# Turns into two other PSUM banks at the opening of the first chunk period, and another place in VectorE's order for the subtractions of the first up tiles

## The chip, the cores and the metric

The kernel runs on one core of a Trainium2 chip. A core has a TensorE (PE: matmuls and transposes, with its weight loads shown as PEld), a VectorE (DVE), a ScalarE (ACT), a GpSimd (POOL) and a SyncE (SP), which here issues the loads from HBM. Each engine works through its own queue in order; semaphores make one engine wait for another. TensorE writes to PSUM, which has eight banks of 128 x 512 fp32. The metric is the device time of one execution in microseconds (us); lower is better. The times before are the median of three runs, 1123.79 us (1122.62 to 1124.88).

## The reference, cut to what matters

One hybrid decoder layer for 256 tokens of width 2048, in fp32:

```
h   = RMSNorm(x)
p   = h @ w_in                              # heads of attention and of a gated recurrence
m   = concat[RMSNorm(attention), recurrence] @ w_out
x   = x + RMSNorm(m)                        # "x2" in the kernel
h   = RMSNorm(x)
u   = relu(h @ w_up)                        # 2048 -> 8192
y   = (u * u) @ w_down                      # 8192 -> 2048
out = x + RMSNorm(y)
```

The change lies behind the layer's first half: where `h` of the MLP is made from `x2`, where the first products with `w_up` start, and where the first products with `w_down` start.

## The kernel before, in words

**Precision.** Each fp32 matmul is done as three faster ones: a value is split in a high part (`whi`, a cast on ScalarE, L90 or L689) and a low part (`wlo`, the value less its high part, a subtraction on VectorE, L91 or L694). `three` and `product` then issue high x high, high x low and low x high. So every tile of weights passes through ScalarE and VectorE before TensorE can take it: a load on SP into a raw buffer, a cast, a subtraction.

**Turns.** TensorE needs activations with their features on the partitions. `turn_act` (and `turn`, `turn_sum`, which call it) transposes four 128 x 128 blocks into one PSUM bank (L637), ScalarE casts the bank to the high part (L639), and VectorE subtracts to get the low part (L640). `turn_u` does the same for `u`: transposes (L669), a square on ScalarE (L671), a cast (L673), a subtraction (L674). A bank is free for the next turn when its last reader is done: for `turn_act` the subtraction on VectorE, for `turn_u` the square on ScalarE.

**PSUM.** The eight banks have four tags: "pj" with three, "sc" with three, "tr" and "o" with one each. `bank(tag, bufs)` gives a bank of a tag; a matmul into it waits until it is free.

**An order written out by hand.** From the last quarter of the `w_out` product on, the program puts TensorE's queue, and then also VectorE's, ScalarE's and SP's, in exactly the order in which the Python code issues the instructions (`manual_schedule`). Where a line stands in the code is where its instruction stands in its engine's queue.

**The up opening (about 400 to 441 us).** `residual(tb)` makes `x2` for 128 tokens (block row `tb`) with its sums of squares; `scaled(tb, c)` (L704, VectorE) makes block `c` of the normed `h` of that row; `turn(tb, c)` turns it into `h2T[c]`. Meanwhile the first four tiles of `w_up` (numbers 0 to 3) are split: `cast_t(i, h)` casts half `h` of tile `i` (L689), `lo_t(i, h)` subtracts it (L694), and with the second half of tile `i` also issues the load of tile `i + 3` (L78), whose raw buffer is the one that tile `i` gives free: three raw buffers go round. `cast2(i)` and `lo2(i)` do both halves. TensorE meanwhile ends the last `w_out` product (`w3`), with the turns of row 0 between its pieces, and goes on with `part(tb, tile, kind)`: four matmuls of one row with one tile, of kind "hh" (high x high), "lh" or "hl" (high x the tile's low part), all from L730. Tile 3 is needed first by `part(0, 3, "hh")`, tile 4 by the `wide_step` loop behind this stretch (L111 to L113).

**The chunk opening (about 471 to 517 us).** From here the MLP runs in chunks of 1024 features. The up products of a chunk are combined from seven products of half size, whose inputs are sums of blocks of `h` (`turn_sum` with the names "s1" to "s4"; "s4" is written into one half of `h2T[0]` and `h2T[1]`, beside the "a11" half that the first products read). `period(ch, ...)` lists a chunk's segments. Each segment has its weights (`prepare` casts and subtracts them, two segments ahead), additions between weight tiles (`adds`, VectorE, L873), turns that stand ahead of its matmuls in TensorE's queue (`turns`), its matmuls (`product`, L869, or `down_half`, L111 to L113), and loads behind them. Before the first period `down_half(0, 0, 0)` has begun the first two sums of the down product in two "sc" banks. They stay in use until the other half of that product has been added (`dn[0][1]`, the third segment) and copied out.

The first period (`ch == 1`) opens with: the first segment (`m1_first[0]`), ahead of it two turns of "s4" and the turn of `u[1, 0]`; the second segment (`m1_first[1]`), ahead of it the turn of `u[1, 1]`; `dn[0][1]`; `m5[0]`, `m5[1]`; `dn[1][0]`; `m6[0]`, `m6[1]`; `dn[1][1]`. In VectorE's queue the "s4" subtractions stand behind the subtractions of the first three segments' weights and one addition.

Of the kernel before, what the change touches and what calls it, by code (L numbers as in the profile page):

```python
# [29 lines left out]
def tile_hybrid_layer(  # L30
# [36 lines left out]
    def nm(s):  # L67
        uid[0] += 1
        return f"{s}{uid[0]}"
# [564 lines left out]
    def turn_act(src, hi, lo, tag="sc", bufs=3):  # L634
        ps = bank(tag, bufs)
        for i in range(4):
            nc.tensor.transpose(ps[:, i * P:(i + 1) * P], src[:, i * P:(i + 1) * P], ident)  # L637
        ps = ps.rearrange("p (a t) -> p a t", a=4)
        nc.scalar.copy(out=hi, in_=ps)  # L639
        nc.vector.tensor_tensor(out=lo, in0=ps, in1=hi.bitcast(F32), op=ALU.subtract)  # L640

    def turn(tb, c):
        turn_act(hn[tb][:, c * 512:(c + 1) * 512], *(h2T[c][:, :, i, tb * P:(tb + 1) * P] for i in range(2)))

    for c in range(3):
        ch = load_wide(w_out_v, 0, c * 512)
# [19 lines left out]
    def turn_u(uT, cb, tb, u, tag, bufs):  # L666
        tp = bank(tag, bufs)
        for i in range(4):
            nc.tensor.transpose(tp[:, i * P:(i + 1) * P], u[:, i * P:(i + 1) * P], ident)  # L669
        u2 = upool.tile([P, 4, P], F32, tag="u2", name=nm("u2"), bufs=2)  # L670
        nc.scalar.activation(out=u2, in_=tp.rearrange("p (a t) -> p a t", a=4), func=AF.Square)  # L671
        hi, lo = (uT[cb][:, :, i, tb * P:(tb + 1) * P] for i in range(2))
        nc.scalar.copy(out=hi, in_=u2)  # L673
        nc.vector.tensor_tensor(out=lo, in0=u2, in1=hi.bitcast(F32), op=ALU.subtract)  # L674
# [16 lines left out]
    def lo_t(i, h):  # L691
        k = slice(2 * h, 2 * h + 2)
        hi, lo = up_w[i]
        nc.vector.tensor_tensor(out=lo[:, k], in0=up_raw[i][:, k], in1=hi[:, k].bitcast(F32), op=ALU.subtract)  # L694
        if h == 1:
            load_t(i + 3)
# [5 lines left out]
    def scaled(tb, c):  # L702
        cs = slice(c * 512, (c + 1) * 512)
        nc.vector.scalar_tensor_tensor(out=hn[tb][:, cs], in0=x2[tb][:, cs], scalar=rh[:, tb:tb + 1], in1=gpre[c],  # L704
                                       op0=ALU.mult, op1=ALU.mult)

    ch = load_wide(w_out_v, 0, 3 * 512, pieces=2)
# [18 lines left out]
    def part(tb, tile, kind):  # L726
        for kt in range(4 * tile, 4 * tile + 4):
            a = tok(h2T, kt, tb)[1 if kind == "lh" else 0]
            b = up_w[tile][1 if kind == "hl" else 0][:, kt % 4, :]
            nc.tensor.matmul(ps[tb], lhsT=a, rhs=b, start=kt == 0 and kind == "hh", stop=kt == NKT - 1 and kind == "hl")  # L730

    def cast2(i):
        cast_t(i, 0)
        cast_t(i, 1)

    def lo2(i):
        lo_t(i, 0)
        lo_t(i, 1)


    w3(0, 11)
    scaled(0, 0)
    scaled(0, 1)
    cast2(0)
    turn(0, 0)
    scaled(0, 2)
    w3(11, 13)
    turn(0, 1)
    cast2(1)
    scaled(0, 3)  # L750
    lo_t(0, 0)
    w3(13, 15)
    turn(0, 2)
    w3(15, 16)
    turn(0, 3)
    evac_post(3, 1, banks[1])
    lo_t(0, 1)
    cast2(2)
    uT = new_uT()
    ps += [bank("pj"), bank("pj")]  # L760
# [9 lines left out]
    scaled(1, 1)  # L770
    part(0, 0, "hl")
    part(0, 3, "hh")
    turn(1, 0)
    part(0, 3, "lh")
    scaled(1, 2)
# [3 lines left out]
    turn(1, 2)  # L779
    part(1, 1, "hh")  # L780
    turn(1, 3)
    lo2(1)
    part(1, 2, "hh")
    part(1, 3, "hh")
    for tile_ in range(4):
# [11 lines left out]
    def half(tb, h):  # L797
        return hn[tb][:, h * 1024:(h + 1) * 1024]
# [4 lines left out]
    def turn_sum(src, c, tag="sc", bufs=3):  # L803
        t = sums[src[0]]
        turn_act(src[1][:, c * 512:(c + 1) * 512], *(t(slice(4 * c, 4 * c + 4), i) for i in range(2)), tag, bufs)
# [135 lines left out]
    raws, banks3, us, uTs = {}, {}, {0: prev}, {0: uT}  # L941
# [45 lines left out]
        m1[1].act.append(lambda: copy_out(0, "a", ch))  # L987
        return m1

    def t(ch, cb, tb, dst, tag="sc"):  # L990
        return lambda: turn_u(uTs[dst], cb, tb, us[ch][cb, tb], tag, 3)

    def period(ch, m1_next):
        d = ch - 1
        m5 = [up_seg("X", ch, h, "b", lambda: sums["s1"], True) for h in range(2)]
        m6 = [up_seg("X", ch, h, "a", lambda: sums["s2"], False) for h in range(2)]
        m7 = [up_seg("P", ch, h, "a", lambda: sums["s3"], False) for h in range(2)]
        m3 = [up_seg("Q", ch, h, "b", lambda: sums["s4"], False) for h in range(2)]
        m4 = [up_seg("X", ch, h, "a", lambda: sums["a22"], False) for h in range(2)]
        m2 = [up_seg("R", ch, h, "c", lambda: sums["a12"], True) for h in range(2)]  # L1000
        dn = [[down_seg(d, c, h) for h in range(2)] for c in range(4)]
        if ch == 1:
            q = [None, m1_first[0], m1_first[1], dn[0][1], m5[0], m5[1], dn[1][0], m6[0], m6[1], dn[1][1],
                 m7[0], m7[1], dn[2][0], m3[0], m3[1], dn[2][1], m4[0], m4[1], m2[0], m2[1],
                 m1_next[0], dn[3][0], m1_next[1], dn[3][1]]
        else:
            q = [m5[0], m5[1], dn[0][0], m6[0], m6[1], dn[0][1], m7[0], m7[1], dn[1][0], m3[0], m3[1], dn[1][1],
                 m4[0], m4[1], dn[2][0], m2[0], m2[1], dn[2][1], m1_next[0], dn[3][0], m1_next[1], dn[3][1]]
        A, B, C = ((lambda b=b: banks3[b, ch]) for b in "abc")
        m5[1].act.append(lambda: copy_out(1, "b", ch))  # L1010
        m6[1].act.append(lambda: copy_out(2, "a", ch))
        m7[1].dve.append(comb(ch, (1, 1), ALU.subtract, lambda: scr[1], A))
        m7[1].act.append(relu_in_place(ch, (1, 1)))
        m3[1].dve.append(comb(ch, (1, 0), ALU.subtract, B, lambda: scr[2]))
        m3[1].act.append(relu_in_place(ch, (1, 0)))
        m4[1].act.append(lambda: relu_21(ch))
        m2[1].dve.append(comb(ch, (0, 0), ALU.add, C, lambda: scr[0]))
        m2[1].act.append(relu_in_place(ch, (0, 0)))

        def plus(to, frm, c, h):  # L1020
            return lambda: add(raws[to, c, h], raws[frm, c, h])

        nx = ch + 1


        if ch == 1:
            plan = [(1, "X", "P", ch, 0), (2, "X", "P", ch, 1), (3, "X", "Q", ch, 0), (4, "X", "Q", ch, 1),
                    (6, "P", "Q", ch, 0), (7, "P", "Q", ch, 1), (12, "X", "R", ch, 0), (14, "X", "R", ch, 1),
                    (19, "X", "P", nx, 0), (21, "P", "Q", nx, 0), (22, "X", "P", nx, 1), (23, "X", "Q", nx, 0)]
        else:  # L1030
            plan = [(1, "X", "Q", ch, 1), (2, "P", "Q", ch, 1), (8, "X", "R", ch, 0), (10, "X", "R", ch, 1)]
            if nx < NCH:
                plan += [(17, "X", "P", nx, 0), (19, "P", "Q", nx, 0), (20, "X", "P", nx, 1), (21, "X", "Q", nx, 0)]
        for k, to, frm, c, h in plan:
            q[k].adds.append(plus(to, frm, c, h))
        if ch == 1:
            q[1].turns += [lambda c=c: turn_sum(("s4", half(0, 0)), c) for c in range(2)]
            q[1].turns.append(t(d, 1, 0, d))
            q[2].turns.append(t(d, 1, 1, d))
            loads = [(1, "d", d, 1, 1), (4, "d", d, 2, 0), (7, "d", d, 2, 1),  # L1040
                     (8, "R", ch, 0), (9, "R", ch, 1), (10, "d", d, 3, 0), (11, "Q", nx, 0), (12, "Q", nx, 1),
                     (13, "d", d, 3, 1), (14, "X", nx, 0), (15, "X", nx, 1), (16, "P", nx, 0), (17, "P", nx, 1),
                     (19, "d", ch, 0, 0), (21, "d", ch, 0, 1)]
        else:
            q[0].turns += [t(d, 0, 0, d), t(d, 0, 1, d)]
            q[3].turns.append(t(d, 1, 0, d))
            q[4].turns.append(t(d, 1, 1, d))
            loads = [(0, "d", d, 1, 0), (3, "d", d, 1, 1), (5, "R", ch, 0), (6, "R", ch, 1), (6, "d", d, 2, 0),
                     (9, "d", d, 2, 1), (12, "d", d, 3, 0), (15, "d", d, 3, 1),
                     (17, "d", ch, 0, 0), (19, "d", ch, 0, 1)]  # L1050
            if nx < NCH:
                loads += [(8, "Q", nx, 0), (9, "Q", nx, 1), (11, "X", nx, 0), (12, "X", nx, 1), (14, "P", nx, 0),
                          (15, "P", nx, 1)]
        for k, name, *where in sorted(loads, key=lambda x: (x[0], x[1] == "d")):
            q[k].loads.append(lambda name=name, where=where: (load_down if name == "d" else load_up)(
                *(where if name == "d" else [name] + where)))
        return [x for x in q if x is not None], q
# [10 lines left out]
    for ch in range(1, NCH):  # L1068
        m1 = first_products(ch + 1) if ch < NCH - 1 else [None, None]
        part, q = period(ch, m1)  # L1070
# [96 lines left out]
```

## Time and profile before

| | before |
|---|---|
| median of three runs | 1123.79 us (1122.62 to 1124.88) |
| the profiled execution's own time | 1124.23 us |
| its span in the profile | 1122.5 us |
| mean granted clock of TensorE | 0.985 of full speed |
| HBM read, written | 204.51 MB, 4.19 MB |

The profile shows one execution. Times in its timeline are us from the span's start: start, duration, engine, line of the program, operation, output <- input, shape; in square brackets the idle time of that engine just before, and what ended it. Durations of grouped rows (x2, x4, ...) run from the first start to the last end. A stretch's row gives, in this order, its bounds, its length, the busy time of PE, PEld, DVE, ACT and POOL (with how many instructions), the granted clock of TensorE (1.00 is full speed), the DMA engines' share and GB/s; the rows of TensorE alone leave the other engines out. Matmuls overlap by a fraction of their length, so 24 of them take less time than 24 times the duration of one.

### The profile page before, as it was taken

Reading aid. Unit: us, or ns where it says so; the run is one execution under the profiler, and the core shown is the slowest. Engines: PE = TensorE matmul, PEld = TensorE weight load, DVE = VectorE, ACT = ScalarE, POOL = GpSimd, SP = SyncE. Lnnn points to the kernel's source line nnn. Section 1 sums busy time; section 2 is a strip of 40 time slices with the busy share of each in tenths; the row PEclk is TensorE's granted clock in tenths of the full one; section 3 lists DMA queues with packets and bytes.
Section 4 is the critical chain, followed back from the end, with each engine's and each line's share of the span. In section 5 each row is a group of like instructions: output and inputs, shape, how many; then the busy total and the mean of one; then the engine's idle time right before and its main releaser. Section 6 shows DMA issues by size and latency. Waiting matters only on the chain.

```text
span 1122.5 us, 14032 instructions
## 1 busy us (share of the span) xinstructions
PE 1088.4 (97%) x5708; PEld 928.5 (83%) x5708; DVE 846.4 (75%) x765; ACT 623.0 (55%) x719; POOL 19.1 (2%) x48
## 2 busy tenths in 40 slices
PE   9999999999999989879999999999999999999996
PEld 8999789999988867658788888888888888888885
DVE  6755666665655457578898898898898898898565
ACT  6655655546454353445665565565565575575542
POOL 2100000000000000000000000000000000000000
PEclk9999989999999999979999999999999999999998
DMA  8743414444468635816727727728628628634662
GB/s 278 245 155 121 153 66 151 151 151 152 149 202 319 209 132 184 303 38 215 246 102 268 257 76 273 251 78 279 243 88 280 232 96 282 222 107 156 231 256 75
DMA packets 125538, 209.61 MB, mean 187 GB/s; under 512 B 3945, under 2 KB 49570, under 8 KB 124450
## 3 DMA queue, kind: packets, MB, share of 16 engines
q1 hardware_dynamic: 125474, 208.72, 54.5%
q8 instruction: 45, 0.74, 0.3%
q14 instruction: 19, 0.16, 0.0%
HBM read 204.51 MB, written 4.19 MB: 186 GB/s over the span
## 4 chain that ended last, share of the span: by engine, by line
PE 90%; DVE 3%; DMA 3%; ACT 2%; issue 1%; SPq 0%; POOL 0%; DVEq 0%; POOLq 0%; ACTq 0%
PE pj L869 22%; PE pj L112 10%; PE pj L113 10%; PE pj L111 10%; PE sc L113 8%; PE sc L111 8%; PE sc L112 8%; DVE wlo L91 2%; PE o L112 1%; PE tr L113 1%; PE o L113 1%; PE tr L112 1%; PE tr L111 1%; ACT whi L90 1%; PE o L111 1%; PE sc L669 1%
## 5 line engine op out<-in xcount | busy, mean ns | idle before, releaser
L91 DVE TENSOR_TENSOR wlo<-raw,whi 128x2048 fp32r<-128x2048 f32 (+2 forms) x77 | 145.6, 1901 | 72.5 <-ACT whi L90 71.3
L90 ACT CAST whi<-d 128x2048 fp32r<-128x2048 f32 x59 | 112.9, 1913 | 113.5 <-PE sc L113 78.9
L91 DVE TENSOR_TENSOR wlo<-d,whi 128x2048 fp32r<-128x2048 f32 x59 | 135.1, 2289 | 49.2 <-ACT whi L90 49.2
L90 ACT CAST whi<-raw 128x2048 fp32r<-128x2048 f32 (+2 forms) x77 | 121.8, 1596 | 80.9 <-PE pj L113 33.2
L90 ACT CAST whi<-X 128x2048 fp32r<-128x2048 f32 x56 | 107.2, 1915 | 88.4 <-DVE X L873 31.4
L111 PE MATMUL sc<-whi,uT 128*128 128x512 f32 x384 | 149.5, 389 | 0.0
L113 PE MATMUL sc<-whi,uT 128*128 128x512 f32 x384 | 149.4, 389 | 0.0
L112 PE MATMUL sc<-wlo,uT 128*128 128x512 f32 x384 | 149.4, 389 | 0.0
L869 PE MATMUL pj<-whi,hT 128*128 128x512 f32 x448 | 145.7, 394 | 0.0
L91 DVE TENSOR_TENSOR wlo<-X,whi 128x2048 fp32r<-128x2048 f32 x56 | 127.9, 2284 | 14.2 <-ACT whi L90 14.2
L112 PE MATMUL pj<-hT,whi 128*128 128x256 f32 x384 | 111.4, 290 | 0.0
L113 PE MATMUL pj<-hT,wlo 128*128 128x256 f32 x384 | 110.6, 288 | 0.4 <-DVE wlo L91 0.3
L111 PE MATMUL pj<-hT,whi 128*128 128x256 f32 x384 | 110.5, 288 | 0.4 <-DVE zq L431 0.4
L869 PE MATMUL pj<-whi,a 128*128 128x512 f32 x336 | 109.8, 395 | 0.0
L869 PEld LDWEIGHTS pj<-whi,hT 128*128 128x128 f32 x448 | 85.2, 190 | 17.8
L869 PE MATMUL pj<-wlo,hT 128*128 128x512 f32 x224 | 88.1, 393 | 0.0
L112 PEld LDWEIGHTS sc<-wlo,uT 128*128 128x128 f32 x384 | 72.1, 188 | 15.1
L113 PEld LDWEIGHTS sc<-whi,uT 128*128 128x128 f32 x384 | 72.1, 188 | 14.9
L111 PEld LDWEIGHTS sc<-whi,uT 128*128 128x128 f32 x384 | 72.1, 188 | 14.9
L91 DVE TENSOR_TENSOR wlo<-P,whi 128x2048 fp32r<-128x2048 f32 x32 | 73.3, 2290 | 13.9 <-ACT whi L90 13.9
L111 PEld LDWEIGHTS pj<-hT,whi 128*128 128x128 f32 x384 | 74.2, 193 | 1.1 <-DVE zq L431 0.7
L113 PEld LDWEIGHTS pj<-hT,wlo 128*128 128x128 f32 x384 | 74.3, 193 | 0.8 <-DVE wlo L91 0.8
(268 smaller groups left out, 2050.1 us busy)
## 6 DMA issues: line engine op xcount, KB each, us to landing
d<-in_w_down_dram SPq DMA_DIRECT2D x59, 1024.0 KB, 5.0
P<-in_w_up_dram SPq DMA_DIRECT2D x28, 1024.0 KB, 5.7
raw<-in_w_in_dram SPq DMA_DIRECT2D x24, 1024.0 KB, 5.2
raw<-in_w_in_dram SPq DMA_DIRECT2D x35, 512.0 KB, 4.5
raw<-in_w_out_dram SPq DMA_DIRECT2D x16, 1024.0 KB, 5.1
X<-in_w_up_dram SPq DMA_DIRECT2D x14, 1024.0 KB, 5.4
Q<-in_w_up_dram SPq DMA_DIRECT2D x14, 1024.0 KB, 5.4
raw<-in_w_up_dram SPq DMA_DIRECT2D x8, 1024.0 KB, 5.4
```

The costliest lines, as they stand in the source:

```text
L90: nc.scalar.copy(out=hi[:, k], in_=raw[:, k])
L91: nc.vector.tensor_tensor(out=lo[:, k], in0=raw[:, k], in1=hi[:, k].bitcast(F32), op=ALU.subtract)
L111: nc.tensor.matmul(o, lhsT=ah, rhs=bh, start=first, stop=False)
L112: nc.tensor.matmul(o, lhsT=ah, rhs=bl, start=False, stop=False)
L113: nc.tensor.matmul(o, lhsT=al, rhs=bh, start=False, stop=last)
L669: nc.tensor.transpose(tp[:, i * P:(i + 1) * P], u[:, i * P:(i + 1) * P], ident)
L869: nc.tensor.matmul(o, lhsT=a, rhs=b, start=fresh and kt == 0 and i == 0, stop=kt == 7 and i == 2, skip_group_check=not fresh)
```

## The change

Two edits in the hand-written order and one in the choice of banks.

In the up opening all four `scaled(0, c)` stand together at the start; the two halves of `lo_t(0, ...)` stand around the first turn of row 0 (they stood behind the fourth scaling and behind `evac_post`); and `lo2(1)` stands ahead of the first turn of row 1 (it stood behind the last). With each `lo_t(i, 1)` goes the load of tile `i + 3` on SP.

In the chunk opening the two turns of "s4" go to "tr" and "o" instead of "sc", and the turn of `u[1, 1]` goes to "tr"; the turn of `u[1, 0]` stays in "sc".

```diff
     w3(0, 11)
-    scaled(0, 0)
-    scaled(0, 1)
+    for c in range(4):
+        scaled(0, c)
     cast2(0)
+    lo_t(0, 0)
     turn(0, 0)
-    scaled(0, 2)
+    lo_t(0, 1)
     w3(11, 13)
     turn(0, 1)
     cast2(1)
-    scaled(0, 3)
-    lo_t(0, 0)
     w3(13, 15)
     turn(0, 2)
     w3(15, 16)
     turn(0, 3)
     evac_post(3, 1, banks[1])
-    lo_t(0, 1)
     cast2(2)
...
     part(0, 3, "hh")
+    lo2(1)
     turn(1, 0)
...
     turn(1, 3)
-    lo2(1)
     part(1, 2, "hh")
...
-    def t(ch, cb, tb, dst, tag="sc"):
-        return lambda: turn_u(uTs[dst], cb, tb, us[ch][cb, tb], tag, 3)
+    def t(ch, cb, tb, dst, tag="sc", bufs=3):
+        return lambda: turn_u(uTs[dst], cb, tb, us[ch][cb, tb], tag, bufs)
...
         if ch == 1:
-            q[1].turns += [lambda c=c: turn_sum(("s4", half(0, 0)), c) for c in range(2)]
+            q[1].turns += [lambda c=c: turn_sum(("s4", half(0, 0)), c, ("tr", "o")[c], 1) for c in range(2)]
             q[1].turns.append(t(d, 1, 0, d))
-            q[2].turns.append(t(d, 1, 1, d))
+            q[2].turns.append(t(d, 1, 1, d, "tr", 1))
```

## The prediction

> **What bounds the kernel now.** First the page: TensorE's share, then, below it, who TensorE waited for.
>
> ```profile
> PE 1088.4 (97%) x5708; PEld 928.5 (83%) x5708; DVE 846.4 (75%) x765; ACT 623.0 (55%) x719; POOL 19.1 (2%) x48
> ```
>
> TensorE (PE) is busy for 97% of the span, so only its gaps and its slow matmuls can be won. The view of waits, PE alone, names the gaps:
>
> ```profile
> PE sc L637 <- DVE hT L640: 11.2, 1, 11.2
> PE pj L730 <- ACT whi L689: 3.7, 2, 3.5
> ...
> PE sc L669 <- DVE hT L640: 1.4, 1, 1.4
> PE pj L112 <- DVE wlo L91: 1.3, 1, 1.3
> ...
> PE o L112 <- DVE wlo L91: 0.7, 1, 0.7
> ```
>
> The columns are the whole wait in us, how often, and the longest. The first four, 17.6 us, lie in two places that the diff touches: the opening of the up projection (400 to 441 us; the 3.7 and the 1.3) and that of the first chunk period (471 to 517; the 11.2 and the 1.4). The table of stretches adds the clock of the second:
>
> ```profile
> 471.50:495.02 23.52, 10.96 (x42) 8.55 (x41) 14.22 (x9) 11.72 (x12) 0.00 (x0) 0.64 0.29 95
> 495.02:516.80 21.78, 21.78 (x98) 18.02 (x96) 21.74 (x12) 13.39 (x11) 0.00 (x0) 1.00 0.15 49
> ```
>
> In the first row PE is busy for 10.96 of 23.52 us at a granted clock of 0.64. In the second PE and VectorE (DVE) are both full: there TensorE cannot come earlier than VectorE does.
>
> **First part: the up opening.** The timeline, by engine (DVE, then SP, ACT, PE):
>
> ```profile
> 403.45 1.42 DVE L704 SCALAR_TENSOR_TENSOR hn<-x,rh,gpre 128x512 f32<-128x512 f32 x2 [0.67 <-POOL rh L629]
> ...
> 409.80 1.28 DVE L640 TENSOR_TENSOR hT<-sc,hT 128x512 fp32r<-128x512 f32 x2
> ...
> 411.60 1.22 DVE L694 TENSOR_TENSOR wlo<-raw,whi 128x1024 fp32r<-128x1024 f32 x1
> 412.73 0.15 DVE L599 TENSOR_TENSOR rf<-pss,ppart 128x1 f32<-128x1 f32 x1
> ...
> 418.13 1.41 DVE L704 SCALAR_TENSOR_TENSOR hn<-x,rh,gpre 128x512 f32<-128x512 f32 x2 [0.66 <-POOL rh L629]
> ...
> 428.49 6.89 DVE L694 TENSOR_TENSOR wlo<-raw,whi 128x1024 fp32r<-128x1024 f32 x6
> ```
> ```profile
> 412.88 0.37 SPq L78 DMA_DIRECT2D raw<-in_w_up_dram  x1
> ...
> 430.90 10.04 SPq L78 DMA_DIRECT2D raw<-in_w_up_dram  x4
> ```
> ```profile
> 416.37 0.63 ACT L589 ACTIVATE junk<-x 128x512 f32<-128x512 f32 x1
> ...
> 418.44 1.99 ACT L689 CAST whi<-raw 128x1024 fp32r<-128x1024 f32 x2 [1.34 <-DMA raw<-in_w_up_dram]
> ...
> 436.31 1.92 ACT L90 CAST whi<-raw 128x2048 fp32r<-128x2048 f32 x1 [8.46 <-DMA raw<-in_w_up_dram]
> ```
> ```profile
> 415.01 1.07 PE L730 MATMUL pj<-wlo,hT 128*128 128x512 f32 x4
> 419.53 0.73 PE L730 MATMUL pj<-whi,hT 128*128 128x512 f32 x2 [3.46 <-ACT whi L689]
> ...
> 426.59 0.63 PE L637 MATMUL sc<-ident,hn 128*128 128x128 f32 x4
> ...
> 440.60 0.50 PE L112 MATMUL pj<-wlo,hT 128*128 128x512 f32 x1 [1.27 <-DVE wlo L91]
> ```
>
> The raw buffer of up tile 3 is that of tile 0, so its load (412.88) stands behind tile 0's second subtraction (411.60). The cast of tile 3 stands behind its landing (418.44), and TensorE from 416.08 to 419.53 behind that cast. Likewise tile 1's subtractions (the first two of the six from 428.49) hold tile 4's load (430.90), its cast (436.31), its subtraction, and TensorE at 440.60.
>
> Nothing is added: the same instructions stand in another order. From 403.45 VectorE now does four scalings at 0.71, to 406.3; a tile subtraction (6.89 / 6 = 1.15) to 407.4; block 0's subtraction (1.28 / 2 = 0.64) to 408.1; the second tile subtraction to 409.2; block 1's to 409.85. The next two start at 409.8 as now, since ScalarE's order, which feeds them, is unchanged. What block 0's later end (408.1) could hold is the transpose of block 3, which takes its bank: that one runs after 409. So 1.15 leaves the way to the step at 412.73: it runs at 411.6, and all behind it up to 418.13 is 1.1 earlier.
>
> SP's queue keeps its order (tile 3's load, the store of x2, tile 4's load); the loads only find their buffers free sooner. Tile 3's load issues at about 409.3. With today's 5.54 (412.88 to 418.42, the cast's wait) it lands at 414.8; ScalarE's squares end at 417.0 - 1.1 = 415.9, and these now end last. The cast runs 416.0 to 418.0, and its first half lets TensorE go at 417.05: the gap shrinks from 3.46 to 1.0, with some 0.5 more before the second half.
>
> Then the scalings of block row 1 end at 418.4 and tile 1's subtractions run to 420.7, ahead of the turns' own. This is the one added delay: the first turn's subtraction and the third scaling wait for them, so the third turn finds its input at 422.0, TensorE standing there for 0.9. I add TensorE's list up at full clock: the fourth turn begins at 423.5 where it began at 426.59. That is **3.1 us** earlier. Tile 4's load issues at 420.8 and lands near 426.3; its subtraction stands behind the other tiles' in VectorE's order and ends by 434.4, before TensorE comes: now at 440.60 - 1.27 less one matmul, 438.9, then at 435.8. The 1.27 goes whole. Next in line is tile 5: its cast follows the relu of the first sum, complete at 434.9, so 0.59 + 1.92 + 2.28 later, at 439.7, it is ready; TensorE needs it 24 matmuls (5.44) and two turns (0.88) after 435.8, at 442.1. That is covered, by 2.4. Sum of the first part: **4.4 us**.
>
> **Second part: the chunk opening.** Times of the profile before, without that shift:
>
> ```profile
> 473.50 0.59 ACT L664 ACTIVATE u<-pj 128x512 f32<-128x512 f32 x1
> ...
> 478.05 0.59 ACT L639 CAST hT<-sc 128x512 fp32r<-128x512 f32 x1
> ```
> ```profile
> 473.62 4.57 DVE L91 TENSOR_TENSOR wlo<-X,whi 128x2048 fp32r<-128x2048 f32 x2 [8.82 <-ACT whi L90]
> ...
> 482.52 0.68 DVE L640 TENSOR_TENSOR hT<-sc,hT 128x512 fp32r<-128x512 f32 x1
> ...
> 488.81 2.28 DVE L873 TENSOR_TENSOR X<-X,P 128x2048 f32<-128x2048 f32 x1
> 493.96 2.29 DVE L91 TENSOR_TENSOR wlo<-X,whi 128x2048 fp32r<-128x2048 f32 x1 [2.86 <-ACT whi L90]
> ...
> 514.51 2.28 DVE L91 TENSOR_TENSOR wlo<-d,whi 128x2048 fp32r<-128x2048 f32 x1
> ```
> ```profile
> 483.26 1.12 PE L637 MATMUL sc<-ident,hn 128*128 128x128 f32 x4 [11.16 <-DVE hT L640]
> ```
>
> And the chain of waits, TensorE's pieces in order of time, for the price of a turn and of 24 matmuls at full clock:
>
> ```profile
> 491.98 0.44 PE sc L669 x4
> ...
> 500.62 5.44 PE pj L869 x24
> ...
> 511.50 5.44 PE pj L869 x24
> ```
>
> The unfinished `down_half` keeps two "sc" banks, so the four turns share the third, and the second s4 turn waits for the first's subtraction, which is fifth in VectorE's queue (482.52). With "tr" and "o", whose last readers stand far ahead in ScalarE's and VectorE's own queues, both s4 turns run at once, and the turn of `u[1,0]`, in the third "sc" bank, at 474.1 when its relu (473.50) is done. The first products follow: their second matmul needs the wlo of 473.62, done at 475.9, so they end between 478.5 (half of 5.44) and 481 (half clock).
>
> What comes late next is the last turn, of `u[1,1]`: it takes "tr" again, so the wait at 482.52 to 483.26 **stays, with less queued behind it**. Behind it on TensorE stand the second first products, the down half, two m5, the next down half, two m6, then the down half that in the profile begins at 511.50 + 5.44 = 516.94. From 483.26 that is 0.44 + 2.72 + 4 x 5.44 = 24.9 us at full clock: 508.2.
>
> The clock adds to it. In windows of 3.41 us, the step at which the granted clock changes here:
>
> ```profile
> 140.25:143.66 3.41, 1.61 (x13) 1.00 0.74 244
> 143.66:147.07 3.41, 3.03 (x12) 0.50 0.88 301
> ...
> 437.21:440.63 3.42, 2.15 (x11) 1.00 0.98 332
> ...
> 488.42:491.83 3.41, 3.41 (x10) 0.50 0.01 2
> ```
>
> A window 1.61 busy (47%) is followed by half clock, one with 2.15 (63%) not. One with 3.03 (89%) doesn't bring the clock back, a full one does. A gap of 2.3 to 4.8 us ahead of 483.26, with more ahead of it, so most likely leaves half clock there; from then TensorE has no gap, and a whole window ends 3.4 to 6.8 us later. I take 5.1: it loses half, 2.55, and the down half begins at 510.75. Bounds: 509.9 and 511.6; no loss at best; 8.6, as now (483.26 to 491.83), at worst, or 512.5.
>
> VectorE's own list gives a floor. After 482.52 its three subtractions run without pause (3 x 0.64, to 484.45), then what now runs from 488.81 to 516.79, without the 2.86: it ends at 509.6, below 510.75. So the second part brings 516.94 - 510.75 = **6.2 us** (4.4 to 7.2).
>
> The Trainium skill, "TensorE: Matmul & The Clock Gate", section "Why this matters for your kernels", asks only that gaps above about 3 us be avoided, and its Part 1 has the clock back after one busy window of about 3.4 us. By it the loss would be 1.7 and the forecast 0.85 lower. The first window above does not agree: all its gaps together are 1.8 us, and half clock followed.
>
> Past 517 TensorE has one wait of 0.7, and VectorE, the buffers and SP's loads there follow TensorE's ends, so all shifts as a block. Sum: 4.4 + 6.2 = 10.6. The profiled execution, 1124.23 us, would be 1113.6; it lies 0.44 above the median of 1123.79, which gives **1113.2 us**.
>
> **Rivals.**
> - *The clock falls at the up opening too* (1.5 us of gaps in one window, 56%, between the 47% that tripped and the 63% that didn't), or half clock lasts as long as now at the second. Either costs 1.7 to 3.4: 1115 to 1116.6.
> - *The change doesn't do what it says at the second opening.* The first products read `h2T`, whose other half the s4 turns write. If they wait for the second s4 subtraction all the same (483.9), half clock lies over them to 489.3 (2 x 2.72), the cast that takes their buffer (1.92) to 491.2, and VectorE's piece at 493.96 begins 2.8 earlier instead of 7.2: 1117. Against it stand two rows of the up opening:
>
> ```profile
> 427.88 0.69 DVE L640 TENSOR_TENSOR hT<-sc,hT 128x512 fp32r<-128x512 f32 x1 [0.72 <-ACT hT L639]
> ```
> ```profile
> 427.90 4.43 PEld L730 LDWEIGHTS pj<-whi,hT 128*128 128x128 f32 x20 [0.18 <-ACT hT L639]
> ```
>
> TensorE loads the hi half of a tile while VectorE still writes its lo half, so it waits by parts of a tile.
> - *One opening alone counts*, the other's gain meeting a later wait, such as the one of 0.7: 1117.6 or 1119.4.
> - *Slower: half clock stays.* If it lasted from 483.26 over all of the 24.9 us of work, they would take 49.8 and the down half would begin at 533.1: 16.2 late, and with the first part 4.4 early, 1135.6. It turns to a loss once half clock lasts longer than 2 x (10.6 + 2.55) = 26.3 us; now it lasts 8.6 past the restart, gaps included. For it speaks that VectorE is full in that stretch, and a TensorE that it paces has gaps; against it, that at half clock TensorE is the slower one and has none. The same page, section "Seeing it yourself", says that the clock has been seen stuck for over 50 us; no run here shows it.
>
> **How the numbers follow.** Forecast (both openings, 1111.3 to 1115) 0.74; first two rivals 0.13; one opening alone 0.06; nothing to measure 0.03; slower 0.04. The best sum, 4.4 + 7.2, gives 1112.2, and the three runs before reach 1.2 below and 1.1 above their median: 1111.2. At the top I take in the first two rivals and the better single opening: 1117.8. A measurement can tell about 0.2% (2.2 us). Faster 0.93, same 0.03, slower 0.04.
>
> **What would show it.** The waits of PE lose the 11.2 and the 1.3; the 3.7 becomes about 1.5. Tile 3's load issues near 409, tile 4's near 421. The transposes of the last turn still end a wait on hT's L640; the span of stretch two, to the down half, falls from 45.4 to about 39. It is wrong if the first products still start after hT's subtraction, if half clock holds for over 7 us after the restart, or if a wait on L91 of several us appears behind 517.

## The result and the profile after

The changed kernel takes 1113.18 us (median of four runs, 1112.75 to 1114.06); the kernel before, on the same chip, 1123.81. The ratio is 0.9907, with a 95% interval of 0.989 to 0.9924: 10.6 us less. The profiled execution took 1112.79 us, with a span of 1111.1.

TensorE's waits in the changed kernel (whole wait in us, how often, the longest; lines behind the diff have moved, L867 was L869 and L871 was L873):

```profile
PE tr L669 <- DVE hT L640: 4.5, 1, 4.5
...
PE sc L669 <- ACT u L664: 1.6, 1, 1.6
...
PE pj L730 <- ACT whi L689: 1.1, 2, 0.8
...
PE pj L867 <- DVE wlo L91: 0.9, 1, 0.9
PE sc L637 <- DVE hn L704: 0.9, 2, 0.7
...
PE o L112 <- DVE wlo L91: 0.6, 1, 0.6
```

The four waits of 17.6 us have become five of 9.0. The 11.2 and the 1.4 are gone, the 3.7 is 1.1, and the turn of `u[1,1]` waits 4.5 in "tr". New are the 1.6 (that of `u[1,0]` for its relu), the 0.9 of the first products for their wlo, and the up opening's third turn (0.7 of the other 0.9). The wait of 1.3 on tile 4 is gone.

The up opening in the timeline of the changed kernel, SP, then ACT, then PE:

```profile
408.63 0.37 SPq L78 DMA_DIRECT2D raw<-in_w_up_dram  x1
...
420.23 14.21 SPq L78 DMA_DIRECT2D raw<-in_w_up_dram  x4
```
```profile
415.35 1.98 ACT L689 CAST whi<-raw 128x1024 fp32r<-128x1024 f32 x2
```
```profile
416.43 0.74 PE L730 MATMUL pj<-whi,hT 128*128 128x512 f32 x2 [0.85 <-ACT whi L689]
417.38 0.73 PE L730 MATMUL pj<-whi,hT 128*128 128x512 f32 x2 [0.21 <-ACT whi L689]
...
421.57 0.63 PE L637 MATMUL sc<-ident,hn 128*128 128x128 f32 x4 [0.73 <-DVE hn L704]
```

Tile 3's load issues 4.2 us earlier than before, tile 4's 10.7 (0.49 of each is that everything in this profile stands 0.49 earlier). The cast of tile 3 no longer follows its landing (no wait stands at 415.35) but ScalarE's squares. TensorE waits 0.85 + 0.21 for it instead of 3.7.

The chunk opening in the same timeline, DVE, then PE:

```profile
477.33 0.68 DVE L640 TENSOR_TENSOR hT<-tr,hT 128x512 fp32r<-128x512 f32 x1
477.93 0.68 DVE L640 TENSOR_TENSOR hT<-o,hT 128x512 fp32r<-128x512 f32 x1
478.53 0.68 DVE L674 TENSOR_TENSOR uT<-u,uT 128x512 fp32r<-128x512 f32 x1
479.13 2.28 DVE L871 TENSOR_TENSOR X<-X,P 128x2048 f32<-128x2048 f32 x1
...
503.02 2.28 DVE L91 TENSOR_TENSOR wlo<-d,whi 128x2048 fp32r<-128x2048 f32 x1
```
```profile
466.31 0.60 PE L637 MATMUL tr<-ident,hn 128*128 128x128 f32 x4
466.74 0.60 PE L637 MATMUL o<-ident,hn 128*128 128x128 f32 x4
...
469.36 0.47 PE L867 MATMUL pj<-whi,hT 128*128 128x512 f32 x1
470.78 0.50 PE L867 MATMUL pj<-wlo,hT 128*128 128x512 f32 x1 [0.94 <-DVE wlo L91]
...
478.07 1.11 PE L669 MATMUL tr<-ident,u 128*128 128x128 f32 x4 [4.50 <-DVE hT L640]
...
505.60 0.39 PE L111 MATMUL sc<-whi,uT 128*128 128x512 f32 x1
```

Both s4 turns run at once, and the first products begin at 469.36, eight us ahead of the subtractions of hT. At 478.07 TensorE starts again, at half clock (1.11 for a turn that otherwise takes 0.60). The down half that stood at 516.78 begins at 505.60.

### The profile page after: what moved, and what is told of

Read it like the earlier page. It is cut to its first block, busy times and chain, and to the rows that moved or that the text cites. A ratio compares the mean times of both kernels' runs of the same rounds, so it can differ in the third digit from the quotient of the medians.

```text
span 1111.1 us, 14033 instructions
## 1 busy us (share of the span) xinstructions
PE 1085.5 (98%) x5708; PEld 926.3 (83%) x5708; DVE 845.8 (76%) x765; ACT 622.7 (56%) x719; POOL 20.1 (2%) x48
## 4 chain that ended last, share of the span: by engine, by line
PE 90%; DVE 3%; DMA 3%; ACT 2%; issue 1%; SPq 0%; POOL 0%; DVEq 0%; POOLq 0%; ACTq 0%
PE pj L867 22%; PE pj L112 10%; PE pj L111 10%; PE pj L113 10%; PE sc L113 8%; PE sc L112 8%; PE sc L111 8%; DMA raw<-in_w_in_dram 1%; PE o L112 1%; PE tr L113 1%; PE o L113 1%; PE tr L112 1%; PE tr L111 1%; PE o L111 1%; DVE wlo L91 1%; PE pj L730 1%
## 5 line engine op out<-in xcount | busy, mean ns | idle before, releaser
L112 PE MATMUL sc<-wlo,uT 128*128 128x512 f32 x384 | 149.4, 389 | 0.0
L867 PE MATMUL pj<-whi,hT 128*128 128x512 f32 x448 | 145.4, 394 | 0.0
L112 PE MATMUL pj<-hT,whi 128*128 128x256 f32 x384 | 111.0, 289 | 0.0
L867 PE MATMUL pj<-whi,a 128*128 128x512 f32 x336 | 109.8, 395 | 0.0
L867 PEld LDWEIGHTS pj<-whi,hT 128*128 128x128 f32 x448 | 85.2, 190 | 17.7
L867 PE MATMUL pj<-wlo,hT 128*128 128x512 f32 x224 | 88.1, 393 | 0.9 <-DVE wlo L91 0.9
L112 PEld LDWEIGHTS sc<-wlo,uT 128*128 128x128 f32 x384 | 72.1, 188 | 15.0
```

The lines of the kernel that those rows point to most:

```text
L112: nc.tensor.matmul(o, lhsT=ah, rhs=bl, start=False, stop=False)
L867: nc.tensor.matmul(o, lhsT=a, rhs=b, start=fresh and kt == 0 and i == 0, stop=kt == 7 and i == 2, skip_group_check=not fresh)
```

## Where the time went, in three stretches

The start of an execution differs by more than 1 us between profiles of these kernels: the second turn of row 0 begins between 405.49 and 407.06. So I measure each profile from that turn. Three stretches: from it to the first s4 turn (the up opening and what follows), from there to the second down half (the chunk opening), and the rest. Four of the rows behind this table, stretches of the kernel before and of the changed one (length in us, busy time of PE, PEld, DVE, ACT and POOL, the granted clock, DMA):

```profile
406.14:471.50 65.36, 60.41 (x287) 48.91 (x286) 42.87 (x47) 29.29 (x40) 1.09 (x2) 0.97 0.64 224
471.50:516.78 45.28, 32.72 (x138) 26.57 (x136) 35.95 (x20) 25.12 (x22) 0.00 (x0) 0.81 0.22 73
```
```profile
405.65:466.31 60.66, 58.87 (x287) 47.85 (x286) 41.80 (x46) 29.07 (x40) 1.08 (x2) 1.00 0.68 241
466.31:505.60 39.29, 32.24 (x137) 26.08 (x136) 36.16 (x20) 25.00 (x22) 0.00 (x0) 0.91 0.26 84
```

| profile of | up stretch | chunk opening | rest | median time, us | ratio to before (95%) |
|---|---|---|---|---|---|
| before | 65.36 | 45.28 | 605.7 | 1123.81 | |
| changed | 60.66 | 39.29 | 605.5 | 1113.18 | 0.9907 (0.989 to 0.9924) |
| order of the up opening alone | 60.63 | 45.31 | 605.5 | 1119.65 | 0.9966 (0.9953 to 0.9979) |
| banks alone | 65.45 | 39.37 | 605.7 | 1118.21 | 0.995 (0.9934 to 0.9967) |
| tile 0's move alone | 61.40 | 44.04 | 605.6 | 1119.66 | 0.9965 (0.9954 to 0.9977) |
| tile 1's move alone | 63.21 | 44.17 | 605.7 | 1121.71 | 0.9981 (0.9972 to 0.999) |
| last turn in "pj" | 60.63 | 38.32 | 605.6 | 1112.43 | 0.9894 (0.9879 to 0.9909) |
| the same, one addition less | 60.66 | 36.03 | 605.5 | 1109.91 | 0.9873 (0.9858 to 0.9888) |
| filling matmuls | 60.58 | 37.70 | 605.7 | 1111.69 | 0.9891 (0.9874 to 0.9907) |
| one bank more | 60.64 | 42.76 | 605.7 | 1117.15 | 0.9938 (0.9923 to 0.9953) |
| changed, once more | 60.63 | 38.37 | 605.6 | 1113.44 | 0.991 (0.9893 to 0.9926) |
| scalings first, last turn in "pj" | 59.92 | 38.30 | 605.4 | 1111.84 | 0.9893 (0.9879 to 0.9908) |
| scalings first, filling matmuls | 59.93 | 37.70 | 605.7 | 1111.35 | 0.989 (0.9876 to 0.9905) |

The times come from four comparisons, in which the kernel before took 1123.81 us (the changed kernel), 1123.89 (the next four rows), 1124.39 (the four after them) and 1123.78 (the last three). Each ratio is to the kernel before of the same comparison.

The change takes 4.70 us out of the first stretch and 5.99 out of the second, together 10.69, and the rest stays the same to 0.3 us in all thirteen profiles: whatever is won or lost ahead of 517 us reaches the end whole.

## The experiments

### The up opening alone

The changed kernel, with the banks of before:

```diff
-            q[1].turns += [lambda c=c: turn_sum(("s4", half(0, 0)), c, ("tr", "o")[c], 1) for c in range(2)]
+            q[1].turns += [lambda c=c: turn_sum(("s4", half(0, 0)), c) for c in range(2)]
             q[1].turns.append(t(d, 1, 0, d))
-            q[2].turns.append(t(d, 1, 1, d, "tr", 1))
+            q[2].turns.append(t(d, 1, 1, d))
```

> Only the new order in the up opening, the banks of the chunk opening as before. Theory A (the two openings pay independently, and nothing behind 517 us takes a gain back): TensorE reaches the chunk opening 4.7 us earlier, that opening still takes 45.4 us from its first turn to the second down half, and the time is 1123.8 - 4.7 = 1119.1. Theory B (one opening's gain meets a later wait, so the gain needs both): the chunk opening becomes longer by what the up opening gave, and the time stays within 1 us of 1123.8.

Measured: 1119.65 us, and an up stretch of 60.63, as in the changed kernel; the chunk opening (45.31) and its wait of 11.2 are those of before:

```profile
467.69 0.60 PE L637 MATMUL sc<-ident,hn 128*128 128x128 f32 x4
479.46 1.11 PE L637 MATMUL sc<-ident,hn 128*128 128x128 f32 x4 [11.17 <-DVE hT L640]
```

TensorE's two rows stand about 4 us earlier than before, and the gap between them is unchanged. The gain isn't given back: theory A. (By the median alone this run and that of tile 0's move, 1119.65 and 1119.66, can't be told apart; by their stretches they can.)

### The banks alone

The kernel before with the other half of the diff (`t` with `bufs`, the turns in "tr", "o" and "tr").

> Only the new banks, the up opening as before. Theory A: the up opening keeps its waits of 3.7 and 1.3 us; the chunk opening takes 39.5 us instead of 45.4, half clock lasts 3.4 to 6.8 us behind the restart, and the time is 1123.8 - 6.0 = 1117.8. Theory B: the wait of 0.7 behind 517 us or a later one grows by several us, and the time is above 1121.

Measured: 1118.21 us, chunk opening 39.37, up stretch 65.45. Half clock held until 489.1, 5.5 us behind the restart at 483.57. Theory A. The two parts alone bring 4.7 and 5.9 in their stretches, and together 10.7: they add up.

### Tile 0's move alone, tile 1's move alone

For tile 0's move alone the changed kernel, with the banks of before and with tile 1's subtractions back behind the last turn:

```diff
     part(0, 3, "hh")
-    lo2(1)
     turn(1, 0)
...
     turn(1, 3)
+    lo2(1)
     part(1, 2, "hh")
```

For tile 1's move alone the kernel before, with only this:

```diff
     part(0, 3, "hh")
+    lo2(1)
     turn(1, 0)
...
     turn(1, 3)
-    lo2(1)
     part(1, 2, "hh")
```

> Of the up opening only the move of tile 0's subtractions (with the four scalings of row 0 together); tile 1's stand behind the last turn, and the banks are as before. Theory A: tile 3's load issues near 408.7, TensorE's wait on L689 falls from 3.7 to about 1.1 and half clock behind it goes; tile 4's load follows the turns and so moves too, and TensorE's wait on L91 stays at 1.3. Gain 3.9 us, time 1119.9. Theory C (the move of tile 1 carries the gain, as tile 4's load would hold TensorE anyway): the wait on L91 grows from 1.3 to about 5, time about 1123.8.

> Of the up opening only the move of tile 1's subtractions ahead of the turns of row 1; the rest is as before. Theory A: they fall into VectorE's idle time while TensorE waits for tile 3, delay nothing, and take away the wait of 1.3 us on L91: time 1122.5. With the other move done they cost TensorE 0.7 ahead of the third turn, so the two moves together bring 4.7 and not 3.9 + 1.3. Theory C: the move brings most of the 4.7, time about 1119.5.

Measured by the up stretch: 65.36 - 61.40 = 3.96 us for tile 0's move (expected 3.9), 65.36 - 63.21 = 2.15 for tile 1's (expected 1.3). With tile 0's move alone tile 4's load follows the turns (it issued at 426.69, before at 430.90), so that its wait stays, at 1.4 instead of growing to 5:

```profile
PE pj L112 <- DVE wlo L91: 1.4, 1, 1.4
...
PE pj L730 <- ACT whi L689: 1.1, 2, 0.8
```

Theory A for the one. For the other the size was off by 0.85. The wait of 1.3 did go, but by the fourth turn of row 1 this profile was already 0.6 ahead. Tile 3's wait was 3.3 instead of 3.7, as its load took 5.37 us to the cast and not 5.56, and half clock ended earlier against the restart. The edit leaves tile 3's load where it was, and the profile of the banks alone, whose up opening is that of before, also has 3.5 instead of 3.7 (its fourth turn is not ahead). So most of the 0.85 is put down to differences between profiles. That is not shown: the ten executions of this kernel lie between 1119.64 and 1122.87 us, and their median is 2.18 below that of the kernel before.

The two moves together bring 4.7 and not 3.96 + 2.15: the 0.6 is not put down to the move, and with both moves the third turn's wait of 0.73 comes in, which neither has alone (3.96 + 2.15 - 0.6 - 0.73 = 4.78).

### The last turn in "pj", and one addition less

```diff
-            q[2].turns.append(t(d, 1, 1, d, "tr", 1))
+            q[2].turns.append(t(d, 1, 1, d, "pj"))
```
```diff
# the second run, besides
-            plan = [(1, "X", "P", ch, 0), (2, "X", "P", ch, 1), (3, "X", "Q", ch, 0), ...
+            plan = [(1, "X", "P", ch, 0), (3, "X", "Q", ch, 0), ...
```

> The changed kernel, with the turn of u[1,1] in a 'pj' bank instead of 'tr', so that it doesn't wait for the first s4 subtraction. The stretch from the first s4 turn to the second down half is 45.4 us before and 39.45 after the change. Theory A (TensorE's restart and half clock cost what VectorE's list leaves them, VectorE is the floor): the wait of 4.5 us goes, TensorE meets VectorE's floor instead (small waits on L674 and L91), and the stretch becomes 37.9; time 1113.2 - 1.5 = 1111.7. Theory D (the 4.5 us wait and the half clock behind it are the whole loss): the stretch falls to about 32, time about 1106.

> As the run before, and the addition of the second half of P to X in the first period (one instruction of VectorE, 2.2 us) is left out, which changes the output. Theory A (VectorE is the floor): the stretch falls by another 2.2 us, to 35.7, time about 1109.5. Theory D: VectorE has room, nothing more is gained.

The first: 1112.43 us, chunk opening 38.32. TensorE with the last turn in "pj":

```profile
475.86 0.60 PE L669 MATMUL pj<-ident,u 128*128 128x128 f32 x4
...
480.14 0.50 PE L113 MATMUL sc<-whi,uT 128*128 128x512 f32 x1 [0.45 <-DVE uT L674]
...
485.14 0.50 PE L113 MATMUL sc<-whi,uT 128*128 128x512 f32 x1 [1.99 <-DVE uT L674]
```

The wait of 4.5 is gone, the turn runs at full clock (0.60), and in its place TensorE waits for VectorE's next subtractions. That is theory A's floor, 0.4 higher than expected; theory D's 32 is far off. How much this bank brings is less sure: the changed kernel's second profile had 38.37 with "tr". By the medians it is 0.75 us (1113.18 and 1112.43, in two comparisons), and 1.3 if each is first taken from the kernel before of its own comparison.

The second run takes one VectorE instruction out of that list, so that its output is not that of the layer. The opening is 2.29 us shorter again (38.32 to 36.03; 2.2 expected), the time 2.5 us. VectorE's last piece and TensorE's second down half, in the first run and then in the second:

```profile
502.87 2.29 DVE L91 TENSOR_TENSOR wlo<-d,whi 128x2048 fp32r<-128x2048 f32 x1
```
```profile
505.49 0.39 PE L111 MATMUL sc<-whi,uT 128*128 128x512 f32 x1
```
```profile
500.08 2.29 DVE L91 TENSOR_TENSOR wlo<-d,whi 128x2048 fp32r<-128x2048 f32 x1
```
```profile
502.65 0.39 PE L111 MATMUL sc<-whi,uT 128*128 128x512 f32 x1
```

In both, VectorE has no wait from the first products' subtractions (469.30 and 468.75) to the end of this piece, and TensorE begins the down half 0.3 us behind it. This is the sharpest reading of the study: once the 4.5 us wait is gone, **VectorE's list sets the pace**, to the instruction. In the changed kernel itself it is not yet so. There TensorE has no wait between 478.07 and 505.60, and VectorE waits twice, 0.97 us in all, for casts that stand behind TensorE:

```profile
491.43 2.29 DVE L91 TENSOR_TENSOR wlo<-d,whi 128x2048 fp32r<-128x2048 f32 x1 [0.48 <-ACT whi L90]
494.21 2.29 DVE L91 TENSOR_TENSOR wlo<-X,whi 128x2048 fp32r<-128x2048 f32 x1 [0.49 <-ACT whi L90]
```

### Filling the gap

```diff
         x.pe(x.w)
+        if k == 0:
+            filler = bank("pj")
+            for i in range(18):
+                product_a = sums["a11"]
+                nc.tensor.matmul(filler, lhsT=product_a(0, 0), rhs=x.w[0][:, i % 4, :], start=True, stop=True)
```

> The changed kernel, with 18 matmuls of no use (into a free 'pj' bank) behind the first products, in the 4.5 us in which TensorE waits: about 4.1 us of work that keeps TensorE busy, so that the granted clock should not fall. Theory A: half clock goes, TensorE passes the second products and the down half 2.7 us earlier and meets VectorE's floor, so 1.5 us is gained: stretch 37.9, time 1111.7. Theory E (half clock costs nothing here because VectorE paces this stretch anyway): stretch 39.45, time 1113.2.

Measured: 1111.69 us, chunk opening 37.70. The timeline of TensorE:

```profile
474.99 4.26 PE L1131 MATMUL pj<-whi,hT 128*128 128x512 f32 x18
479.09 0.60 PE L669 MATMUL tr<-ident,u 128*128 128x128 f32 x4
```

The turn behind the filler takes 0.60 and not 1.11: the clock is full there. (In this profile half clock came earlier, from 470.43 to 473.85, over the first products, and was gone before the filler began.) With 18 useless matmuls the opening is 1.6 us shorter than in the first profile of the changed kernel and 0.7 shorter than in the second. Theory A: half clock costs something here, and VectorE's floor stops the gain: from 468.70 to 504.44, the end of its piece for that down half, VectorE's rows have no wait.

### One bank more instead of two

```diff
-            ... turn_sum(("s4", half(0, 0)), c, ("tr", "o")[c], 1) for c in range(2)]
+            ... turn_sum(("s4", half(0, 0)), c, ("tr", "sc")[c], (1, 3)[c]) for c in range(2)]
```

> The changed kernel, but only the first s4 turn leaves 'sc' (for 'tr'); the second stays in the third 'sc' bank, and the turn of u[1,0] behind it waits for its subtraction. Theory A: the first products start only behind the second s4 subtraction, at half clock, and the cast that takes their buffer comes late; the stretch is about 42.6, time about 1116.3. Theory F (one bank more is enough, as only the second s4 turn's wait was long): stretch 39.5, time 1113.2.

Measured: 1117.15 us, chunk opening 42.76. The timeline, DVE and PE:

```profile
477.75 0.68 DVE L640 TENSOR_TENSOR hT<-sc,hT 128x512 fp32r<-128x512 f32 x1
...
486.07 2.29 DVE L91 TENSOR_TENSOR wlo<-X,whi 128x2048 fp32r<-128x2048 f32 x1 [2.25 <-ACT whi L90]
```
```profile
466.56 0.60 PE L637 MATMUL sc<-ident,hn 128*128 128x128 f32 x4
478.49 1.12 PE L669 MATMUL sc<-ident,u 128*128 128x128 f32 x4 [11.33 <-DVE hT L640]
```

The second s4 turn now runs at once and nothing is won by that: the 11 us wait moves on to the next turn that needs the bank. What is won, 2.5 of the 6.0, is that the subtractions of hT run without a turn between them. In the kernel before, VectorE waited there:

```profile
485.03 0.69 DVE L640 TENSOR_TENSOR hT<-sc,hT 128x512 fp32r<-128x512 f32 x1 [1.83 <-ACT hT L639]
```

The late first products still cost VectorE a wait of 2.25 for their buffer (2.86 before). These two are 2.44 less waiting. Theory A.

### A version that is faster still

All four scalings of row 1 ahead of `lo2(1)`, with the last turn in "pj" or with the filler, beside the changed kernel:

```diff
     cast2(3)
-    scaled(1, 0)
-    scaled(1, 1)
+    for c in range(4):
+        scaled(1, c)
...
-    scaled(1, 2)
...
-    scaled(1, 3)
```

> The changed kernel once more, beside the two below on one chip: 1113.2, all theories.

> The changed kernel with the last turn in 'pj' and with all four scalings of row 1 ahead of tile 1's subtractions in the up opening. If TensorE's wait of 0.7 us ahead of the third turn is real loss, as the sum of the first part had it, it goes, and the two add up: 0.7 + 0.8 below the changed kernel, 1111.7. If the bank that the fourth turn takes (free only behind the first turn's subtraction, which is now later) takes the wait's place, only the 0.8 is left: 1112.4.

> The same scalings, with the 18 filling matmuls instead of the 'pj' bank: 0.7 + 1.5 below the changed kernel, 1111.0; if the fourth turn's bank takes the wait's place, 1111.7.

Measured in one comparison: 1113.44 us (1113.14 to 1114.24) for the changed kernel, 1111.84 (1111.56 to 1112.2) with the scalings and "pj", 1111.35 (1110.23 to 1113.16) with the scalings and the filler. The up stretch is 59.92 and 59.93 against 60.63: the third turn's wait of 0.7 was real loss, and the fourth turn's bank doesn't take its place. The "pj" version has all its runs below all runs of the changed kernel; the intervals of the ratios to before overlap. Of its 1.60 us, 0.71 is the up stretch, so by these medians the bank of the last turn brings about 0.9. It needs no useless work and is the one to keep.

## Why the prediction was right

Forecast 1113.2, measured 1113.18. The mechanism was right in both openings. That the two agree to 0.02 us is luck: the first part came 0.3 larger than its term and the second 0.2 smaller, and the kernel's own runs lie between 1112.75 and 1114.06. (The lower end of the range has a slip in its sum: 1112.2 - 1.2 is 1111.0, not 1111.2. Nothing hangs on it.)

- **First part, 4.4 forecast, 4.70 measured.** Tile 3's load was put at 409.3 and tile 4's at 420.8, in the times of before; they issued at 408.63 and 420.23, with everything in this profile 0.49 earlier (405.65 against 406.14). That ScalarE's squares end last in place of the landing was right (no wait at 415.35). The gaps were smaller than forecast (0.85 + 0.21 instead of 1.0 + 0.5, the third turn's 0.73 instead of 0.9), but that changed nothing: the third turn waits for VectorE, and the fourth began at 423.46 in the times of before, where it was put at 423.5. The 0.3 lies behind it. A row of before, then three of the changed kernel:

```profile
438.94 0.39 PE L111 MATMUL pj<-whi,hT 128*128 128x512 f32 x1
```
```profile
422.97 0.60 PE L637 MATMUL sc<-ident,hn 128*128 128x128 f32 x4
...
435.26 0.39 PE L111 MATMUL pj<-whi,hT 128*128 128x512 f32 x1
435.49 0.39 PE L112 MATMUL pj<-wlo,hT 128*128 128x512 f32 x1
```

  Before, the matmul behind the wait on tile 4 began 1.66 after its predecessor (438.94 to 440.60), now 0.23. So this stop cost 1.43 and not its idle time of 1.27, since matmuls that don't stop overlap (0.39 each, 0.23 apart). That is half of the 0.3; the rest is spread over the matmuls up to the s4 turn.
- **Second part, 6.2 forecast, 5.99 measured.** The opening of the changed kernel was put at 39.25 us (510.75 - 471.50) and is 39.29. The 0.2 is in the kernel before, whose down half begins at 516.78 and not at 516.94. The last turn's wait stayed where it was put: 478.07 is 11.76 behind the first s4 turn, as in the profile before (483.26 - 471.50). What was won is what no longer stands behind it: two turns and the first products (0.44 + 0.44 + 2.72 = 3.6), the wait of 1.40, and some 0.9 of half clock (8.6 us with 1.4 of idle time in them before, 5.4 now, each costing half). This estimate gives 5.9.
- **The clock.** At the up opening it did not fall, so the first half of the first rival did not come: the granted clock is 1.00 from 405.65 to 466.31. The gaps of the first window there came to 1.06 us and not 1.5 (2.35 of 3.41 busy, 69%). Half clock behind the restart was forecast at 5.1 us. It ended at 483.49, 5.4 later, and not 8.6 as in the second half of that rival:

```profile
476.66:483.49 6.83, 5.42 (x15) 0.50 0.46 154
```

  This row of the changed kernel is two windows of 3.41 us, all at half clock. The Trainium skill, "TensorE: Matmul & The Clock Gate", Part 1, has windows of that length that run free of the kernel; this trace agrees on the length, in that the clock fell at 476.66 and came back 6.83 later, two whole windows. That 5.1 was so near is luck too: in the second profile of the changed kernel half clock behind the restart lasted 3.4 us (below). And how busy a window must be to bring the clock back is not settled here. The prediction's window of 3.03 us (89%) did not, but in the filler's profile the one from 470.43 to 473.85, busy for 2.80 us (82%), did.
- **VectorE's floor.** Forecast 509.6 in the times of before, that is 38.1 behind the first s4 turn; VectorE's last piece ended at 503.02 + 2.28 = 505.30, 39.0 behind it. The 0.9 is the two waits of 0.97 for casts, which the forecast did not have; without them the list takes 38.0, as forecast. In the first run with "pj" and in the filler's, where VectorE has no wait, the same piece ended 38.0 and 37.9 behind the first s4 turn. So from 39.29 the bank and the filler had about 1.4 us to win.
- **Independent halves of h2T.** The rival in which the first products wait for hT fell: they began at 469.36, the first of those subtractions at 477.33.
- **The block behind 517.** The rest of the kernel is the same in all profiles, 605.4 to 605.7; the wait of 0.7 on L112 is 0.6 now. The rivals in which a later wait takes the gain, or half clock stays, did not come.

## What to carry to other kernels

When a wait in a queue written by hand can't be moved, ask what stands behind it that doesn't need it: two idle banks let 3.6 us of turns and matmuls pass ahead of a wait that stayed, and a second wait and some half clock went with them. Free all the buffers of such a chain at once, or the wait only moves to the next one that needs the last buffer (one bank brought 2.5, two 6.0). And before paying to remove the next wait, add up the list of the engine that would come next: here VectorE's left 0.7 to 1.6 us, by the profile of the changed kernel that is taken.

## What was not expected

The same kernel's chunk opening differs by 0.9 us between two profiles of the changed kernel (39.29 and 38.37), and the one of before by 1.3 between its variants (45.31, 44.04, 44.17). The second profile of the changed kernel in windows of 3.41 us:

```profile
468.98:472.39 3.41, 1.34 (x7) 1.00 0.85 277
472.39:475.80 3.41, 3.41 (x10) 0.51 0.01 3
475.80:479.22 3.42, 0.51 (x2) 0.99 0.01 2
479.22:482.63 3.41, 3.41 (x10) 0.51 0.89 273
```

Here the windows lay so that most of the gaps of 1.6 and 0.9 ahead of the first products fell into one (39% busy). Half clock followed, and cleared behind the next. The 2.9 us wait then brought it again, for 3.4 us only, as TensorE started right at a window's edge, at 479.22. Neither of the two gaps that brought it the first time is longer than 2 us. In both profiles TensorE restarts 11.76 us behind the first s4 turn; in the first the nearest edge of a window lies 10.35 behind that turn, in the second 11.76. Half clock lasted 5.42 and 3.41 us behind the restart, and half of that difference, 1.0 us, is what separates the two openings (0.92). So where the windows lie against the work decides about 1 us per execution in this kernel, and a change of that size can't be read from one profile. What shifts the start of an execution by over 1 us ahead of 406 us was not tried.
